# The last down chunk's second token tile in two halves of 256 columns, and both halves of every layer norm centred before either is scaled

## The chip, the cores and the metric

The kernel runs on one core of one Trainium2 chip. The metric is the device time of one execution in microseconds (us). The time before is 1677.98 us, the median of three runs. The engines are TensorE (PE, with its weight loads shown apart as PEld), VectorE (DVE), ScalarE (ACT), GpSimd (POOL) and SyncE (SP), which issues nearly all transfers.

## The reference

Two layers of a decoder trunk work on 256 tokens of 1024 channels in f32. Each layer is a half-step SwiGLU feed-forward network (FFN), a mixer of three parallel branches, and a second half-step FFN. After each of these six stages stands a residual sum with a layer norm:

```
for l in range(DEPTH):
    x = layer_norm(ALPHA * x + 0.5 * swiglu(x, ffn1_up[l], ffn1_down[l]), ln1_g[l], ln1_b[l])
    mix = hybrid_mixer(x, positions, w_in[l], ...)
    x = layer_norm(ALPHA * x + mix, ln2_g[l], ln2_b[l])
    x = layer_norm(ALPHA * x + 0.5 * swiglu(x, ffn2_up[l], ffn2_down[l]), ln3_g[l], ln3_b[l])

def layer_norm(x, gain, bias):
    mu = mean(x); var = mean((x - mu) ** 2)
    return (x - mu) * rsqrt(var + LN_EPS) * gain + bias
```

Up projections have 2 x 2816 columns, down projections go from 2816 channels back to 1024, and the mixer ends in an output projection of 1024 by 1024. The kernel keeps 2x + f and a larger epsilon where the reference has x + 0.5 f, which a layer norm does not tell apart.

## The kernel before

The 256 tokens are two token tiles of 128, `t = 0` and `t = 1`; `x[t]` is 128 tokens by 1024 channels. The weights are cut into chunks of 512 columns, and a chunk into units of up to four blocks of 128 rows (`k`). A unit is loaded (`ws`), rounded on ACT to a high part (`wh`, L280) and its rest taken on DVE as a low part (`wl`, L290), each some 2 us for a full unit. Activations have the same two parts: `xT` and `hT` are pairs of a high and a low tile, channels on partitions. Each product is the sum of three matmuls in fp32r: low by `wh`, high by `wl`, high by `wh`. All of them are issued in `mm_unit` (L321) into an accumulator `acc` of one PSUM bank of 512 columns; three such banks rotate.

`parts` says how a unit is laid out. In the form `tokens`, 128 tokens are the stationary operand and 512 weight columns move; the down and output projections use it. In the form `channels`, 128 weight columns are stationary and the 256 tokens move. A third case is the second half of the chunk `bkv`, which has the form `tokens` with 256 moving columns.

A down projection is two chunks (`n = 0, 1`) of 22 blocks of rows. When the last unit of a chunk is done for a token tile, `done_down` (or `done_out` after the mixer) calls `residual`: x is scaled and the accumulator added (L466), and `bn_stats` takes the statistics of these 512 columns (L467). After `n = 1` it calls `norm`: `bn_aggr` (L472), epsilon (L474), the power -0.5 on POOL (L475), and then for each half of 512 columns two steps: subtract the mean and multiply by the gain (L479), multiply by the power and add the bias (L480). L480 needs the power, L479 does not.

The order of the work is the order of the code; every engine takes its instructions in that order. Between two stages the last W = 3 units are run for tile 0 first, then for tile 1, so that tile 0's norm and transposes lie under tile 1's matmuls. `x_transposes(t)` transposes each half of x on PE (L458, into the bank T for the first 512 channels and S for the second), and `split` makes `xT` of it on ACT (L448) and DVE (L449). Tile 0 is transposed ahead of the last unit of tile 1. Tile 1 is transposed in the middle of the next stage's third unit for tile 0:

```
for u in (s, s + 1):
    self.mm_unit(u, 0)
self.mm_unit(s + 2, 0, lambda: (self.x_transposes(1), self.hi_until(s + W)))
```

After the mixer the last chunk has only two units, since it has eight blocks of rows. So the three last units span two chunks there, and tile 1's residual of the first of them falls on DVE right after tile 0's norm. After the last stage there are no transposes: SP stores each half of each tile of x (L1104) as soon as its L480 is done.

Of the kernel before, what the change touches and what calls it, by code (L numbers as in the profile page):

```python
# [34 lines left out]
F32 = mybir.dt.float32  # L35
# [4 lines left out]
OP = mybir.AluOpType  # L40
# [4 lines left out]
ALPHA = float(np.float32((2.0 * DEPTH) ** 0.25))  # L45
EPS = float(np.float32(1e-5))
# [115 lines left out]
class Kernel:  # L162
# [131 lines left out]
    def mm_unit(self, u, t, mid=None, tick=False):  # L294
        nc = self.nc
        c, k0, n, _ = self.units[u]
        ch = self.chunks[c]
        if ch["ps"][t] is None:
            ch["ps"][t] = self.acc.tile([128, 512], F32, name="acc")
        ps = ch["ps"][t]  # L300
        wh, wl = self.ready[u]
        if k0 == 0 and t == 0:
            if ch["kind"] == "avf" and ch["arg"] == 2:
                assert self.b_done == 4
                self.queue_yT(1, 8)
            elif ch["kind"] == "proj" and ch["arg"] == (1, 1):
                self.queue_yT(2, 8)
            elif ch["kind"] == "gate" and ch["arg"] == (0, 0):
                self.drain()
                self.queue_yT(0, 6)  # L310
        ch["left"][t] -= 1
        parts = self.parts(ch, t)
        for i, (c0, c1, f) in enumerate(parts):
            for k in range(n):
                if mid and k == n // 2:
                    mid()
                pairs = f(k0 + k, wh[:, k], wl[:, k])
                for j, (a, b) in enumerate(pairs):
                    first = k0 + k == 0 and i == 0 and j == 0
                    last = ch["left"][t] == 0 and k == n - 1 and j == 2  # L320
                    nc.tensor.matmul(ps[:, c0:c1], a, b, start=first, stop=last, skip_group_check=len(parts) > 1)  # L321
        if tick:
            self.tick(t)
        if ch["left"][t] == 0:
            getattr(self, "done_" + ch["kind"])(ch, t, ps)
            ch["ps"][t] = None


    def parts(self, ch, t):

        kind = ch["kind"]

        def pairs(k):
            if kind == "down":
                return self.hT[0][:, k], self.hT[1][:, k]
            if kind in ("proj", "out"):
                hi, lo = (self.mT if kind == "out" else self.yT[ch["arg"][0]])[k // 4]
                return hi[:, k % 4], lo[:, k % 4]
            return self.xT[0][:, k], self.xT[1][:, k]

        def tokens(i, order, c0=0, c1=512):
            def f(k, wh, wl):
                h, l = (order(v, i) for v in pairs(k))
                return (l, wh[:, c0:c1]), (h, wl[:, c0:c1]), (h, wh[:, c0:c1])
            return f

        def channels(b):
            def f(k, wh, wl):
                h, l = pairs(k)
                c = slice(128 * b, 128 * b + 128)  # L350
                return (wl[:, c], h), (wh[:, c], l), (wh[:, c], h)
            return f

        nat = lambda v, i: v[:, 128 * i:128 * i + 128]
        if kind in ("cq", "ck", "bq", "aqk", "gate", "proj") or kind == "up" and ch["arg"] > 1 or kind == "bkv" and t == 0:
            return [(256 * b, 256 * b + 256, channels(2 * t + b)) for b in range(2)]
        if kind == "bkv":
            return [(256 * i, 256 * i + 256, tokens(i, nat, 256)) for i in range(2)]
        return [(0, 512, tokens(t, nat))]


    def setup(self):
        nc, a = self.nc, self.a
        self.x = [self.per.tile([128, 1024], F32, name=f"x{t}") for t in range(2)]
        self.ident = self.per.tile([128, 128], F32, name="ident")
        load = lambda t, n: nc.sync.dma_start(self.x[t][:, 512 * n:512 * n + 512],
                                              a["x"][128 * t:128 * t + 128, 512 * n:512 * n + 512])
        nc.scalar.dma_start(self.ident, a["ident"])
        load(0, 0)
        self.dma_early(0, 0)  # L370
        load(0, 1)
        for k in range(1, 4):
            self.dma_early(0, k)
        load(1, 0)
        load(1, 1)
        for v in (1, 2):
            for k in range(4):
                self.dma_early(v, k)
        self.dma_until(self.STAGE - 1)
        self.xT = [self.per.tile([128, 8, 256], F32R, name=f"xT{i}") for i in range(2)]  # L380
        self.mask = self.per.tile([128, 640], F32, name="mask")
        self.sink = self.per.tile([128, DEPTH, HB], F32, name="sink")
        self.nhalf = self.per.tile([128, 8], F32, name="nhalf")
        nc.vector.memset(self.nhalf, -0.5)
        self.cos = self.per.tile([128, 256], F32, name="cos")
        self.sin = self.per.tile([128, 256], F32, name="sin")
        self.gbias = self.per.tile([128, DEPTH, 3, 8], F32, name="gbias")
        self.st = [self.per.tile([128, 2, 6], F32, name=f"st{t}") for t in range(2)]

    def warm_up(self, n):  # L390

# [68 lines left out]
            self.split(sl(self.xT[0]), sl(self.xT[1]), ps)  # L460


    def residual(self, t, n, ps, scale):
        nc = self.nc
        xs = self.x[t][:, 512 * n:512 * n + 512]
        nc.vector.scalar_tensor_tensor(xs, xs, scale, ps, op0=OP.mult, op1=OP.add)  # L466
        nc.vector.bn_stats(self.st[t][:, n], xs)  # L467

    def norm(self, t, eps):
        nc = self.nc  # L470
        mv = self.sml.tile([128, 2], F32, name="mv")
        nc.vector.bn_aggr(mv, self.st[t])  # L472
        rs = self.sml.tile([128, 1], F32, name="rs")
        nc.vector.tensor_scalar(rs, mv[:, 1:2], eps, None, op0=OP.add)  # L474
        nc.gpsimd.tensor_tensor(rs, rs, self.nhalf[:, 0:1], op=OP.pow)  # L475
        for n in range(2):
            sl = slice(512 * n, 512 * n + 512)
            xs = self.x[t][:, sl]
            nc.vector.scalar_tensor_tensor(xs, xs, mv[:, 0:1], self.g[:, sl], op0=OP.subtract, op1=OP.mult)  # L479
            nc.vector.scalar_tensor_tensor(xs, xs, rs, self.b[:, sl], op0=OP.mult, op1=OP.add)  # L480


# [684 lines left out]
```

## Time and profile before

| what | before |
|---|---|
| median of 3 runs (lowest, highest) | 1677.98 us (1677.12, 1678.56) |
| profiled execution: its own time, and its span from first to last instruction | 1677.88 us, 1676.1 us |
| PE busy | 1662.5 us, 99% of the span, 12325 matmuls |
| DVE busy, ACT busy, POOL busy | 63%, 49%, 3% |
| granted TensorE clock, mean | 0.998 of full speed |
| read from memory | 297.31 MB, 178 GB/s |

The own time is 1.78 us longer than the span, which is what lies around the first and the last instruction. Busy PE is a share of time in which some matmul was under way, not of its peak. What the table does not tell is where PE waits in short places and what lies behind its last matmul.

### The profile page before, as it was taken

The numbers are of one execution on the slowest core, as the hardware profiler recorded it, in microseconds if no ns is written. First come the engines' busy times: TensorE is split into PE (matmuls) and PEld (weight loads), VectorE is DVE, ScalarE is ACT, GpSimd is POOL, SyncE is SP. The second block draws the span as 40 slices with busy tenths as digits, with TensorE's granted clock in tenths as the row PEclk, the third lists the DMA queues.
The fourth block names the chain that finished last, engine by engine and source line by source line (L and its number), as shares of the span: only waits on it lengthen the run. The fifth ranks groups of instructions, "written<-read, shape, count | busy, mean of one in ns | idle before, by whom it ended". The sixth has DMA issues, their size and how long they took to land.

```text
span 1676.1 us, 29127 instructions
## 1 busy us (share of the span) xinstructions
PE 1662.5 (99%) x12325; PEld 1530.6 (91%) x12325; DVE 1063.5 (63%) x1532; ACT 829.6 (49%) x1195; POOL 53.7 (3%) x124
## 2 busy tenths in 40 slices
PE   9999999999999999999999999999999999999997
PEld 7998899998999997999889988999989999989986
DVE  5554668878765467545564456788778555674544
ACT  5443343566776644443344344335667864544431
POOL 0000000000111000000000000000001110000000
PEclk9999999999999999999999999999999999999999
DMA  8544554444543454655445455445444534545451
GB/s 291 200 189 189 201 202 171 156 164 158 176 171 137 179 190 176 225 190 193 172 178 224 189 197 196 172 153 188 162 164 165 178 138 169 218 167 226 172 206 51
DMA packets 50674, 303.39 MB, mean 181 GB/s; under 512 B 7024, under 2 KB 10352, under 8 KB 16624
## 3 DMA queue, kind: packets, MB, share of 16 engines
q1 hardware_dynamic: 49248, 297.27, 48.3%
q0 software_dynamic: 1152, 4.19, 0.7%
q8 instruction: 97, 1.59, 0.4%
q14 instruction: 33, 0.27, 0.0%
q10 hardware_dynamic: 144, 0.07, 0.0%
HBM read 297.31 MB, written 1.05 MB: 178 GB/s over the span
## 4 chain that ended last, share of the span: by engine, by line
PE 96%; DVE 2%; issue 1%; ACT 1%; DMA 0%; POOL 0%; POOLq 0%; SPq 0%
PE acc L321 89%; PE S L641 1%; PE S L630 1%; PE U L776 1%; PE U L853 1%; PE T L630 1%; DVE x L480 0%; ACT af L650 0%; DVE wl L290 0%; DMA x<-in_x_dram 0%; PE S L458 0%; PE T L682 0%; PE T L641 0%; POOL rs L475 0%; DVE x L466 0%
## 5 line engine op out<-in xcount | busy, mean ns | idle before, releaser
L321 PE MATMUL acc<-xT,wh 128*128 128x256 f32 x4800 | 843.5, 279 | 0.0
L321 PEld LDWEIGHTS acc<-xT,wh 128*128 128x128 f32 x4800 | 732.0, 188 | 0.5
L290 DVE TENSOR_TENSOR wl<-ws,wh 128x2048 fp32r<-128x2048 f32 (+1 forms) x277 | 614.8, 2239 | 176.7 <-ACT wh L280 176.3
L321 PE MATMUL acc<-xT,wl 128*128 128x256 f32 x2400 | 674.6, 281 | 0.0
L280 ACT ACTIVATE wh<-ws 128x2048 fp32r<-128x2048 f32 (+1 forms) x277 | 519.0, 1875 | 255.6 <-PE acc L321 219.1
L321 PEld LDWEIGHTS acc<-xT,wl 128*128 128x128 f32 x2400 | 451.2, 188 | 3.9 <-issue 2.7
L321 PE MATMUL acc<-wh,xT 128*128 128x512 f32 (+1 forms) x832 | 260.7, 390 | 0.3 <-DVE xT L449 0.3
L321 PE MATMUL acc<-wh,hT 128*128 128x512 f32 x704 | 222.0, 395 | 0.0
L321 PEld LDWEIGHTS acc<-wh,xT 128*128 128x128 f32 x832 | 154.8, 189 | 36.3 <-issue 1.3
L321 PE MATMUL acc<-wl,xT 128*128 128x512 f32 (+1 forms) x416 | 161.3, 388 | 0.0
L321 PEld LDWEIGHTS acc<-wh,hT 128*128 128x128 f32 x704 | 132.7, 188 | 30.5
L321 PE MATMUL acc<-wl,hT 128*128 128x512 f32 x352 | 138.9, 395 | 0.0
L321 PE MATMUL acc<-slab,wh 128*128 128x256 f32 x704 | 126.4, 281 | 0.0
L491 DVE TENSOR_TENSOR h<-sa,acc 128x512 f32<-128x512 f32 x36 | 24.7, 687 | 154.3 <-PE acc L321 149.6
L321 PEld LDWEIGHTS acc<-slab,wh 128*128 128x128 f32 x704 | 108.1, 188 | 0.0
L321 PE MATMUL acc<-slab,wl 128*128 128x256 f32 x352 | 100.5, 286 | 0.0
L488 ACT ACTIVATE sa<-acc 128x512 f32<-128x512 f32 x36 | 21.5, 596 | 158.4 <-PE acc L321 158.4
L321 PEld LDWEIGHTS acc<-wl,xT 128*128 128x128 f32 x416 | 78.5, 189 | 16.2
L321 PEld LDWEIGHTS acc<-wl,hT 128*128 128x128 f32 x352 | 66.3, 188 | 15.2
L321 PEld LDWEIGHTS acc<-slab,wl 128*128 128x128 f32 x352 | 66.3, 188 | 0.8 <-issue 0.7
L650 ACT ACTIVATE an<-an,bnm 128x128 f32<-128x128 f32 x64 | 28.4, 446 | 55.8 <-DVE bnm L816 31.8
L466 DVE SCALAR_TENSOR_TENSOR x<-x,acc 128x512 f32<-128x512 f32 x24 | 16.4, 685 | 53.6 <-PE acc L321 53.6
(190 smaller groups left out, 1233.7 us busy)
## 6 DMA issues: line engine op xcount, KB each, us to landing
ws<-in_w_dram SPq DMA_DIRECT2D x265, 1024.0 KB, 4.9
ws<-in_w_dram SPq DMA_DIRECT2D x12, 512.0 KB, 4.0
ws<-in_w_dram SPq DMA_DIRECT2D x12, 256.0 KB, 5.4
va<-slab SPq DMA_DIRECT2D x96, 32.0 KB, 4.0
gain<-in_ln_g_dram SPq DMA_DIRECT2D x4, 512.0 KB, 5.7
gain<-in_ln_b_dram SPq DMA_DIRECT2D x4, 512.0 KB, 7.2
slab<-in_decay_dram POOLq DMA_DIRECT2D x4, 512.0 KB, 4.6
x<-in_x_dram SPq DMA_DIRECT2D x4, 256.0 KB, 6.1
```

The source lines that it names most:

```text
L280: self.nc.scalar.activation(wh[:, :n], self.staged[v][:, :n], AF.Copy)
L290: self.nc.vector.tensor_tensor(wl[:, :n], ws[:, :n], wh[:, :n].bitcast(F32), op=OP.subtract)
L321: nc.tensor.matmul(ps[:, c0:c1], a, b, start=first, stop=last, skip_group_check=len(parts) > 1)
L466: nc.vector.scalar_tensor_tensor(xs, xs, scale, ps, op0=OP.mult, op1=OP.add)
L488: nc.scalar.activation(self.sa, ps, AF.Silu)
L491: nc.vector.tensor_tensor(h, self.sa, ps, op=OP.mult)
L630: nc.tensor.transpose(ps[:, c + 128 * (i - lo):c + 128 * (i - lo) + 128], P[:, 128 * i:128 * i + 128], self.ident)
L641: self.nc.tensor.matmul(Sp[e][:, 128 * t:128 + 256 * t], q[r, 128 * t:128 * t + 128], k[r, :128 * t + 128], start=True, stop=True)
L650: self.nc.scalar.activation(P, P, AF.Exp, bias=nm, scale=0.125, accum_out=den)
L776: mm = lambda out, v, p, first, last: nc.tensor.matmul(out, v, p, start=first, stop=last, skip_group_check=True)
L853: nc.tensor.matmul(u[:, 128 * j:], v[:, j], P[i][:, e, 256 * j:256 + 128 * j], start=j == 0, stop=j == 1, skip_group_check=True)
```

## The change

Three edits. In the last chunk of the kernel (the second layer's second FFN, down, `n = 1`) tile 1 gets two accumulators of 256 columns each. Every unit of it runs its blocks for the first 256 columns and then for the second. After the last unit's first half, `residual` is called for these 256 columns, and after the second half for the others. `bn_stats` now takes 256 columns at a time everywhere: a residual of 512 columns issues two of them, and `bn_aggr` combines four groups instead of two. And `norm` runs L479 for both halves first, then L480 for both. The second and the third edit apply to all twelve norms.

```diff
--- before.py
+++ after.py
@@ -295,8 +295,9 @@
         nc = self.nc
         c, k0, n, _ = self.units[u]
         ch = self.chunks[c]
+        halves = ch is self.chunks[-1] and t == 1
         if ch["ps"][t] is None:
-            ch["ps"][t] = self.acc.tile([128, 512], F32, name="acc")
+            ch["ps"][t] = [self.acc.tile([128, 512], F32, name="acc") for _ in range(1 + halves)]
         ps = ch["ps"][t]
         wh, wl = self.ready[u]
         if k0 == 0 and t == 0:
@@ -318,11 +319,18 @@
                 for j, (a, b) in enumerate(pairs):
                     first = k0 + k == 0 and i == 0 and j == 0
                     last = ch["left"][t] == 0 and k == n - 1 and j == 2
-                    nc.tensor.matmul(ps[:, c0:c1], a, b, start=first, stop=last, skip_group_check=len(parts) > 1)
+                    if halves:
+                        first = k0 + k == 0 and j == 0
+                    nc.tensor.matmul(ps[i * halves][:, c0:c1], a, b, start=first, stop=last, skip_group_check=len(parts) > 1)
+            if halves and ch["left"][t] == 0:
+                self.residual(1, 2 + i, ps[i], 2.0 * ALPHA, 256)
         if tick:
             self.tick(t)
         if ch["left"][t] == 0:
-            getattr(self, "done_" + ch["kind"])(ch, t, ps)
+            if halves:
+                self.norm(1, 4.0 * EPS)
+            else:
+                getattr(self, "done_" + ch["kind"])(ch, t, ps[0])
             ch["ps"][t] = None
 
 
@@ -352,6 +360,8 @@
             return f
 
         nat = lambda v, i: v[:, 128 * i:128 * i + 128]
+        if ch is self.chunks[-1] and t == 1:
+            return [(256 * i, 256 * i + 256, tokens(t, nat, 256 * i, 256 * i + 256)) for i in range(2)]
         if kind in ("cq", "ck", "bq", "aqk", "gate", "proj") or kind == "up" and ch["arg"] > 1 or kind == "bkv" and t == 0:
             return [(256 * b, 256 * b + 256, channels(2 * t + b)) for b in range(2)]
         if kind == "bkv":
@@ -385,7 +395,7 @@
         self.cos = self.per.tile([128, 256], F32, name="cos")
         self.sin = self.per.tile([128, 256], F32, name="sin")
         self.gbias = self.per.tile([128, DEPTH, 3, 8], F32, name="gbias")
-        self.st = [self.per.tile([128, 2, 6], F32, name=f"st{t}") for t in range(2)]
+        self.st = [self.per.tile([128, 4, 6], F32, name=f"st{t}") for t in range(2)]
 
     def warm_up(self, n):
 
@@ -460,11 +470,12 @@
             self.split(sl(self.xT[0]), sl(self.xT[1]), ps)
 
 
-    def residual(self, t, n, ps, scale):
-        nc = self.nc
-        xs = self.x[t][:, 512 * n:512 * n + 512]
-        nc.vector.scalar_tensor_tensor(xs, xs, scale, ps, op0=OP.mult, op1=OP.add)
-        nc.vector.bn_stats(self.st[t][:, n], xs)
+    def residual(self, t, n, ps, scale, size=512):
+        nc = self.nc
+        xs = self.x[t][:, size * n:size * n + size]
+        nc.vector.scalar_tensor_tensor(xs, xs, scale, ps[:, size * n % 512:size * n % 512 + size], op0=OP.mult, op1=OP.add)
+        for i in range(2 * n, 2 * n + 2) if size == 512 else (n,):
+            nc.vector.bn_stats(self.st[t][:, i], self.x[t][:, 256 * i:256 * i + 256])
 
     def norm(self, t, eps):
         nc = self.nc
@@ -473,10 +484,10 @@
         rs = self.sml.tile([128, 1], F32, name="rs")
         nc.vector.tensor_scalar(rs, mv[:, 1:2], eps, None, op0=OP.add)
         nc.gpsimd.tensor_tensor(rs, rs, self.nhalf[:, 0:1], op=OP.pow)
-        for n in range(2):
-            sl = slice(512 * n, 512 * n + 512)
-            xs = self.x[t][:, sl]
+        halves = [(self.x[t][:, sl], sl) for sl in (slice(0, 512), slice(512, 1024))]
+        for xs, sl in halves:
             nc.vector.scalar_tensor_tensor(xs, xs, mv[:, 0:1], self.g[:, sl], op0=OP.subtract, op1=OP.mult)
+        for xs, sl in halves:
             nc.vector.scalar_tensor_tensor(xs, xs, rs, self.b[:, sl], op0=OP.mult, op1=OP.add)
 
 
```

The first place is DVE at the end of the mixer, tile 0 (`x_78`) and the first residual of tile 1 (`x_79`). Before:

```order
L466 SCALAR_TENSOR_TENSOR x_78<-x_78,acc 128x512
L467 BN_STATS st_116<-x_78 128x6
L472 BN_AGGR mv<-st_116 128x2
L474 TENSOR_SCALAR rs<-mv 128x1
L479 SCALAR_TENSOR_TENSOR x_78<-x_78,mv,slab 128x512
L480 SCALAR_TENSOR_TENSOR x_78<-x_78,rs,slab 128x512
L479 SCALAR_TENSOR_TENSOR x_78<-x_78,mv,slab 128x512
L480 SCALAR_TENSOR_TENSOR x_78<-x_78,rs,slab 128x512
L466 SCALAR_TENSOR_TENSOR x_79<-x_79,acc 128x512
L467 BN_STATS st_117<-x_79 128x6
L290 TENSOR_TENSOR wl<-ws,wh 128x2048
L449 TENSOR_TENSOR xT_108<-T,xT_107 128x4x128
```

The same place in the changed kernel, whose line numbers are up to eleven higher:

```order
L476 SCALAR_TENSOR_TENSOR x_78<-x_78,acc 128x512
L478 BN_STATS st_116<-x_78 128x6 x2
L483 BN_AGGR mv<-st_116 128x2
L485 TENSOR_SCALAR rs<-mv 128x1
L489 SCALAR_TENSOR_TENSOR x_78<-x_78,mv,slab 128x512 x2
L491 SCALAR_TENSOR_TENSOR x_78<-x_78,rs,slab 128x512 x2
L476 SCALAR_TENSOR_TENSOR x_79<-x_79,acc 128x512
L478 BN_STATS st_117<-x_79 128x6 x2
L290 TENSOR_TENSOR wl<-ws,wh 128x2048
L459 TENSOR_TENSOR xT_108<-T,xT_107 128x4x128
```

The second centring step has moved ahead of the first scaling step, and a second `bn_stats` stands behind each first one; nothing else has moved there.

The second place is DVE behind the last matmul, tile 1, in the changed kernel; before, it is the first eight rows above with `x_79`.

```order
L476 SCALAR_TENSOR_TENSOR x_79<-x_79,acc 128x256
L478 BN_STATS st_117<-x_79 128x6
L476 SCALAR_TENSOR_TENSOR x_79<-x_79,acc 128x256
L478 BN_STATS st_117<-x_79 128x6
L483 BN_AGGR mv<-st_117 128x2
L485 TENSOR_SCALAR rs<-mv 128x1
L489 SCALAR_TENSOR_TENSOR x_79<-x_79,mv,gain_15413 128x512 x2
L491 SCALAR_TENSOR_TENSOR x_79<-x_79,rs,gain_15414 128x512 x2
```

The first residual of 256 columns and its `bn_stats` now stand ahead of the second pair.

The third place is PE in the middle of the last unit of tile 1, where the first accumulator (`acc_16415`) ends and the second begins:

```order
L324 MATMUL acc_16415<-wh_16482,hT1_15014 128x256
L324 MATMUL acc_16415<-wl_16483,hT0_15013 128x256
L324 MATMUL acc_16415<-wh_16482,hT0_15013 128x256
L324 MATMUL acc_16416<-wh_16482,hT1_15014 128x256
L324 MATMUL acc_16416<-wl_16483,hT0_15013 128x256
L324 MATMUL acc_16416<-wh_16482,hT0_15013 128x256
```

Before, each of the 22 blocks was three matmuls of 512 columns; now it is three of 256 columns for each half, so 66 matmuls have become 132, each with its own weight load.

## Rows read from the trace of the kernel before

**Rows 1.** The page's chain of work that ended last, shares of the span by engine.
```profile
PE 96%; DVE 2%; issue 1%; ACT 1%; DMA 0%; POOL 0%; POOLq 0%; SPq 0%
```
**Rows 2.** PE's weight loads, whom they waited for: us in total, times, longest us.
```profile
PEld acc L321 <- DVE xT L449: 1.2, 2, 0.6
PEld S L458 <- DVE x L480: 0.8, 2, 0.4
```
**Rows 3.** Timeline, PE, from mixer to FFN (layer 0): start us, us, engine, line.
```profile
650.14 0.39 PE L321 MATMUL acc<-wh,slab 128*128 128x512 f32 x1
650.68 0.50 PE L321 MATMUL acc<-wh,xT 128*128 128x512 f32 x1 [0.16 <-DVE xT L449]
651.02 0.39 PE L321 MATMUL acc<-wl,xT 128*128 128x512 f32 x1
...
657.31 0.40 PE L321 MATMUL acc<-wl,xT 128*128 128x512 f32 x1
...
657.78 0.60 PE L458 MATMUL T<-ident,x 128*128 128x128 f32 x4
...
658.96 0.48 PE L321 MATMUL acc<-wh,xT 128*128 128x512 f32 x1
```
**Rows 4.** Timeline, DVE and PE, tile 1 from first FFN to mixer.
```profile
201.51 0.75 DVE L480 SCALAR_TENSOR_TENSOR x<-x,rs,gain 128x512 f32<-128x512 f32 x1 [0.45 <-POOL rs L475]
...
203.45 0.60 PE L458 MATMUL T<-ident,x 128*128 128x128 f32 x4
...
204.25 0.48 PE L321 MATMUL acc<-wh,xT 128*128 128x512 f32 x1
```
**Rows 5.** Timeline, DVE, from mixer to FFN: tile 0, then tile 1's last step.
```profile
643.10 0.74 DVE L479 SCALAR_TENSOR_TENSOR x<-x,mv,slab 128x512 f32<-128x512 f32 x1
...
646.43 0.68 DVE L466 SCALAR_TENSOR_TENSOR x<-x,acc 128x512 f32<-128x512 f32 x1
...
649.94 0.68 DVE L449 TENSOR_TENSOR xT<-T,xT 128x512 fp32r<-128x512 f32 x1
...
657.74 0.75 DVE L480 SCALAR_TENSOR_TENSOR x<-x,rs,slab 128x512 f32<-128x512 f32 x1
```
**Rows 6.** Timeline behind the last matmul: tile 1's residual and norm on DVE and POOL.
```profile
1666.77 0.69 DVE L466 SCALAR_TENSOR_TENSOR x<-x,acc 128x512 f32<-128x512 f32 x1 [3.22 <-PE acc L321]
1667.49 0.69 DVE L467 BATCH_NORM_STATS2 st<-x 128x6 f32<-128x512 f32 x1
1668.22 0.21 DVE L472 BATCH_NORM_AGGREGATE mv<-st 128x2 f32<-128x12 f32 x1
...
1668.54 0.74 DVE L479 SCALAR_TENSOR_TENSOR x<-x,mv,gain 128x512 f32<-128x512 f32 x1
1668.70 0.99 POOL L475 TENSOR_TENSOR rs<-rs,nhalf 128x1 f32<-128x1 f32 x1 [7.38 <-DVE rs L474]
1669.72 0.75 DVE L480 SCALAR_TENSOR_TENSOR x<-x,rs,gain 128x512 f32<-128x512 f32 x1 [0.44 <-POOL rs L475]
1670.39 0.74 DVE L479 SCALAR_TENSOR_TENSOR x<-x,mv,gain 128x512 f32<-128x512 f32 x1
1671.16 0.75 DVE L480 SCALAR_TENSOR_TENSOR x<-x,rs,gain 128x512 f32<-128x512 f32 x1
```
**Rows 7.** Groups of one line each: duration ns min/median/max, first and last start us, forms.
```profile
L952 DVE BATCH_NORM_STATS2 cst<-y x32: 258/260/287, 271.2 to 1126.6; 128x6 f32<-128x128 f32 x32
...
L428 DVE SCALAR_TENSOR_TENSOR ang<-n,ang x4: 414/424/427, 93.9 to 95.3; 128x256 f32<-128x256 f32 x4
...
L321 PEld LDWEIGHTS acc<-wh,hT x704: 187/188/193, 134.1 to 1666.1; 128*128 128x128 f32 x176
```
**Rows 8.** Timeline, PE, 256 moving columns in the form tokens (bkv, layer 1).
```profile
1108.32 0.28 PE L321 MATMUL acc<-wl,xT 128*128 128x256 f32 x1
...
1110.81 0.28 PE L321 MATMUL acc<-wl,xT 128*128 128x256 f32 x1
```
**Rows 9.** Transfers, busy share in tenths from 1670 to 1675 us, 0.125 us a digit.
```profile
DMA  0000000000299999200000889996101000000000
```

## The prediction

> **What bounds the kernel now.** I read the chain of work that ended last first: 96% of the span is PE [rows 1]. So the time changes only where PE waits inside the run, or in what stands behind its last matmul. The change touches the norms and the last chunk, so I asked which of PE's waits name a norm. There are two kinds, each met twice, once in each layer [rows 2]: matmuls that wait for the low part of `xT` (L449), and the transposes of the second half of x into S, which wait for L480. The timeline puts both at the passage from the mixer to the second FFN [rows 3].
>
> The first: between the starts at 650.14 and 651.02 lie 0.88 us where two matmuls of 512 columns take 2 x 0.233 = 0.47 (9 blocks of three matmuls from 651.02 to 657.31 give 6.29 / 27 = 0.233). So 0.41 us is lost. The second: from the first transpose into T to the first matmul behind the S transposes it is 1.18 us (657.78 to 658.96), and 0.80 at a passage without a wait [rows 4]. So 0.38 us is lost. Together that is 0.79 us a layer, 1.58 us in the run, all behind DVE. At the other three passages PE meets no such wait.
>
> At the end [rows 6] DVE starts the last residual at 1666.77 and ends the last L480 at 1671.91: 5.14 us in which nothing else runs, then the last transfer.
>
> **The norm's new order.** L479 does not need the power, L480 does. Before, DVE stood idle 0.44 us ahead of the first L480 and then ran L479, L480 for the second half [rows 6]. From the first L479 (1668.54) to the end of the last L480 (1671.91) it took 3.37 us. Two such steps that do not depend on each other start 0.67 us apart (1669.72, 1670.39). In the new order all four do: the power is there 1.15 us after the first L479 starts (1668.70 + 0.99 - 1668.54), and the first L480 starts at 2 x 0.67 = 1.34. So the norm ends at 3 x 0.67 + 0.75 = 2.76, 0.61 us earlier. The first half is the loser: it ends at 1.34 + 0.75 = 2.09 where it was 1.93, 0.16 us later.
>
> **The split statistics.** No row shows `bn_stats` on 256 columns. On 128 it takes 0.26 [rows 7], on 512 0.69 [rows 6]; a straight line between gives 0.405. Two are 0.81, so 0.12 us more. But two neighbours that do not depend on each other overlap by 0.08 (0.75 long, 0.67 apart), which leaves 0.04. I take 0.04 and keep 0.12. `bn_aggr` on four groups has no row: it lies between the 0.21 of two groups and twice that; I take 0.10 more and keep 0 and 0.21. Seven of the twelve norms end under PE's matmuls, as shown below; the four of the mixers and the last one are in the sums.
>
> **From mixer to FFN.** DVE works through tile 0's norm, tile 1's first residual, a weight split, and then the `xT` for which PE waits, without a pause but the one for the power [rows 5]. From the first L479 (643.10) to the residual (646.43) it was 3.33 us and becomes 4 x 0.67 = 2.68: 0.65 earlier. Against it stand 0.04 and 0.10 for tile 0's statistics and 0.04 for tile 1's. L449 at 649.94 comes 0.47 earlier, at worst (0.12, 0.10, 0.12) 0.31. PE lost 0.41, so the first wait goes, at worst 0.10 us of it stays.
>
> What is late next is tile 1. Its norm starts 0.47 - 0.14 = 0.33 earlier and ends a further 0.61 earlier: the second half of x is ready at 658.49 - 0.94 = 657.55. PE, now 0.41 earlier, begins the T transposes at 657.37 and, about half of the 0.80 us on, the S ones at 657.77. That holds with 0.2 us in hand, so the second wait goes too. The first half of x was ready at about 657.05 (the last L480's start less 1.44 as in rows 6, plus 0.75) and becomes 0.33 - 0.16 = 0.17 earlier, 656.88, ahead of 657.37. Sum: 2 x (0.41 + 0.38) = **1.58 us**, at worst 2 x (0.31 + 0.38) = 1.38.
>
> The later first half must also hold at the other passages. In rows 4 it is ready at 202.26, with statistics and order some 0.30 later, and PE comes to it at 203.45. The cover is 0.9 us; were it gone, each tenth would cost a tenth.
>
> **The last chunk on PE.** 66 matmuls of 512 columns become 132 of 256. The nearest rows are the same form with 256 moving columns [rows 8]: seven blocks in 2.49 us, 2.49 / 21 = 0.1186 for one. Two make 0.2372 against 0.2330: 0.0042 a pair, 66 x 0.0042 = **0.28 us** more. The other end is exact halves, nothing. [...]
>
> The second accumulator must be free when tile 1 comes to its second half in the chunk's first unit. It was read by the 0.69 us residual of the chunk before; since then PE has issued six matmuls of tile 0 (1.4 us) and six of the first half (0.7 us). That covers it; without the cover it would be at most 0.7 us, once.
>
> **Behind the last matmul.** The first half's residual and statistics (0.42 by the same operation on 256 columns [rows 7], and 0.405) lie under the twelve matmuls of the last unit's second half (12 x 0.1186 = 1.42), with DVE idle 3.22 us before [rows 6]. What is left behind the last matmul is 0.69 - 0.42 = 0.27 shorter in L466 and 0.69 - 0.405 = 0.28 in the statistics, 0.10 longer in `bn_aggr`, 0.61 shorter in the norm: 1.06 us. The two last transfers ran apart, each 0.85 us of nearly full engines [rows 9], the second from 0.84 us after its L480. Now they are issued 0.67 apart, so the second waits up to 0.18; I take 0.18 and keep 0. The end gains 1.06 - 0.18 - 0.28 = **0.60 us**.
>
> **Sum.** 1.58 + 0.60 = 2.18 us off the profiled execution's own 1677.88: 1675.7. The median is 0.10 above that execution, less than the three runs differ.
>
> **Rivals.**
> A: the waits in the mixer do not give time back. DVE, which runs earlier, then waits for ACT's high part of a weight, or PE merely stops at the next thing it needs. For it: tile 1's S transposes have 0.2 us in hand only. Against it: the loads and splits are released by the same DVE queue, which is earlier too. Then only the end gains: 1677.3.
> B: the end gains nothing: the last transfer lands no earlier, or the 256-column matmuls cost 0.9 us in place of 0.28, 0.013 a pair. Then 1677.88 - 1.58 = 1676.3.
> C, slower: a weight load takes 0.188 us [rows 7], and if the loads stand alone, 66 more cost 12.4 us: 1677.88 - 2.18 - 0.28 + 12.4 = 1687.8. It decides from 0.037 us a pair on, where both gains are eaten. Against it: in rows 8 each matmul has its own load and they start every 0.1186 us, less than one load lasts. [...]
>
> **Chances.** The forecast 0.77, A 0.12, B 0.08, C 0.03. The best ends of the unknown costs (1.58 and 1.16) give 1675.1, and the three runs lie up to 0.9 from their median, so the range begins at 1674.5; it reaches to A at 1677.3, and leaves out C and some spread at either end. A measurement of this kernel can tell about 0.2%, 3.4 us, from no change. Only the low tail of the forecast lies below 1674.6: faster 0.07. Slower is C and a little more, 0.04. The same 0.89.
>
> **What would show it.** In the changed profile no weight load of PE waits for L459 or L491; T to first matmul takes 0.80 at both mixers; the first L491 has no idle time before it; the last residual to the end of the last L491 takes about 4.1 us where it was 5.14; the last chunk's tile 1 has blocks of about 0.711 us for six matmuls. The forecast is wrong if those waits stay, if six take over 0.73, or if the last transfer still moves data more than 2 us after its L491.

## The result, and the profile after

The changed kernel is slower: 1685.85 us (median of six runs, 1685.54 to 1687.62) against 1677.99 us for six runs of the kernel before beside it, a ratio of 1.0051, with a 95% interval of 1.0041 to 1.0061. The forecast was 1675.7 us, its range ended at 1677.3, and "slower" had a chance of 0.04. The profiled execution has a span of 1683.8 us, where it was 1676.1, at a granted clock of 0.999.

What is strange is that each step that the prediction spoke of happened. I read the same places in the same order. First the page's chain of work that ended last, by engine [rows 1], and the weight loads of PE that waited for DVE in the list of waits [rows 2]:

```profile
PE 98%; ACT 1%; DMA 0%; DVE 0%; issue 0%; SPq 0%; DVEq 0%
```
```profile
PEld T L996 <- DVE slab L459: 1.7, 2, 0.9
...
PEld acc L324 <- DVE wl L459: 0.5, 1, 0.5
```

DVE is gone from the chain. L459 is what L449 was and L491 what L480 was: no load waits for the `xT` of L459 or for the x of L491 any more. Of the two rows with L459 that are left, `T L996` is a wait inside the mixer that was there before (`T L985`, 1.8 us in all), and `wl` is one at the start of the kernel, 9.4 us in. The timeline of PE at the passage from mixer to FFN [rows 3]:

```profile
653.99 0.39 PE L324 MATMUL acc<-wh,slab 128*128 128x512 f32 x1
654.22 0.39 PE L324 MATMUL acc<-wh,xT 128*128 128x512 f32 x1
654.45 0.39 PE L324 MATMUL acc<-wl,xT 128*128 128x512 f32 x1
...
661.21 0.60 PE L468 MATMUL T<-ident,x 128*128 128x128 f32 x4
...
662.00 0.48 PE L324 MATMUL acc<-wh,xT 128*128 128x512 f32 x1
```

From the last `slab` matmul to the second of `xT` it is 0.46 us, two matmuls and no gap (0.88 before), and from the T transposes to the first matmul behind the S ones 0.79 (1.18 before). DVE at the same passage [rows 5]:

```profile
645.90 0.75 DVE L478 BATCH_NORM_STATS2 st<-x 128x6 f32<-128x256 f32 x2
646.69 0.26 DVE L483 BATCH_NORM_AGGREGATE mv<-st 128x2 f32<-128x24 f32 x1
646.99 0.15 DVE L485 TENSOR_SCALAR rs<-mv 128x1 f32<-128x1 f32 x1
647.06 1.41 DVE L489 SCALAR_TENSOR_TENSOR x<-x,mv,slab 128x512 f32<-128x512 f32 x2
648.38 1.41 DVE L491 SCALAR_TENSOR_TENSOR x<-x,rs,slab 128x512 f32<-128x512 f32 x2
649.71 0.68 DVE L476 SCALAR_TENSOR_TENSOR x<-x,acc 128x512 f32<-128x512 f32 x1
```

No idle time stands before L491, and the four steps take 2.65 us where they took 3.33 (forecast 2.68). And the end [rows 6], PE's last matmuls and then DVE:

```profile
1673.07 0.28 PE L324 MATMUL acc<-wl,hT 128*128 128x256 f32 x1
...
1676.28 0.28 PE L324 MATMUL acc<-wl,hT 128*128 128x256 f32 x1
1676.40 0.28 PE L324 MATMUL acc<-wh,hT 128*128 128x256 f32 x1
```
```profile
1676.72 0.42 DVE L476 SCALAR_TENSOR_TENSOR x<-x,acc 128x256 f32<-128x256 f32 x1 [0.54 <-PE acc L324]
...
1679.33 1.41 DVE L491 SCALAR_TENSOR_TENSOR x<-x,rs,gain 128x512 f32<-128x512 f32 x2
```

From the last residual to the end of the last L491 it is 4.02 us, where it was 5.14. Nine triples of 256 columns take 3.21 us, so six matmuls 0.713 (forecast 0.711). Behind L491 it is 3.06 us to the end of the span, where it was 4.19: the two last transfers, which ran apart [rows 9], now run in one stretch (1676 to 1684 us, 0.2 us a digit), and SP's queue, which before waited 2.3 us for the last of them, now waits 0.6 us twice (before, then after):

```profile
DMA  0000000000000000000000002999999600000000
```
```profile
SPq L1163 <- DMA out_dram<-x: 2.3, 1, 2.3
```
```profile
SPq L1174 <- DMA out_dram<-x: 1.2, 2, 0.6
```

From the start of the last matmul to the end of the span it is 7.40 us, and it was 9.76 (1676.1 - 1666.34, its row in the trace of before).

So the time was lost somewhere else. The page's costliest group of PE tells where, first before, then after:

```profile
L321 PE MATMUL acc<-xT,wh 128*128 128x256 f32 x4800 | 843.5, 279 | 0.0
```
```profile
L324 PE MATMUL acc<-xT,wh 128*128 128x256 f32 x4800 | 854.6, 281 | 0.0
```

This group is 11 us longer. With the 2400 `wl` matmuls beside it, it holds the matmuls of the form `channels` that read `xT`: 2400 triples (two with `wh`, one with `wl`) of 256 moving tokens, 1152 of them in the up projections and the others in the mixers. The diff doesn't touch them. In the timeline of the first up projection, before and then after, each row with `wl` marks one triple:

```profile
60.02 0.28 PE L321 MATMUL acc<-xT,wl 128*128 128x256 f32 x1
...
65.97 0.28 PE L321 MATMUL acc<-xT,wl 128*128 128x256 f32 x1
```
```profile
59.73 0.28 PE L324 MATMUL acc<-xT,wl 128*128 128x256 f32 x1
...
65.77 0.28 PE L324 MATMUL acc<-xT,wl 128*128 128x256 f32 x1
```

Both stretches hold 17 triples: 5.95 / 17 = 0.350 us before, 6.04 / 17 = 0.355 after. There is no wait in either; every matmul merely starts 1.8 ns later. The triples of the mixers are slower in both (0.353 and 0.358). Added up over the starts of all 7200 matmuls in the two traces it is 11.0 us. The down projections, whose weights and activations the change moves together, start 0.9 ns later each (232.4 and 233.3 ns), another 0.9 us. With -1.6 at the mixers and -1.9 at the end (7.40 - 9.76, with the 0.12 by which the last matmul has become shorter and the 0.3 for the halves of the last chunk added) that makes +8.4, and +7.9 is measured.

### The profile page after: what moved, and what is told of

Its sections match the earlier page's. It is cut to its first block, busy times and chain, and to the rows that moved or that the text cites. A ratio compares the mean times of both kernels' runs of the same rounds, so it can differ in the third digit from the quotient of the medians.

```text
span 1683.8 us, 29284 instructions
## 1 busy us (share of the span) xinstructions
PE 1672.7 (99%) x12391; PEld 1542.5 (92%) x12391; DVE 1064.2 (63%) x1557; ACT 829.5 (49%) x1195; POOL 53.9 (3%) x124
## 3 DMA queue, kind: packets, MB, share of 16 engines
q0 software_dynamic: 1152, 4.19, 0.8%
## 4 chain that ended last, share of the span: by engine, by line
PE 98%; ACT 1%; DMA 0%; DVE 0%; issue 0%; SPq 0%; DVEq 0%
PE acc L324 92%; PE S L652 1%; PE S L641 1%; PE U L787 1%; PE U L864 1%; PE T L641 1%; ACT af L661 0%; DMA ws<-in_w_dram 0%; PE T L693 0%; PE T L652 0%; PE T L468 0%; PE S L468 0%; ACT wh L280 0%; PE T L518 0%; PE T L996 0%; PE S L934 0%
## 5 line engine op out<-in xcount | busy, mean ns | idle before, releaser
L324 PE MATMUL acc<-xT,wh 128*128 128x256 f32 x4800 | 854.6, 281 | 0.0
L324 PE MATMUL acc<-wh,hT 128*128 128x512 f32 (+1 forms) x748 | 224.3, 382 | 0.0
L324 PEld LDWEIGHTS acc<-wh,hT 128*128 128x128 f32 x748 | 137.5, 188 | 29.7
L324 PE MATMUL acc<-wl,hT 128*128 128x512 f32 (+1 forms) x374 | 142.7, 382 | 0.0
L324 PEld LDWEIGHTS acc<-wl,hT 128*128 128x128 f32 x374 | 70.3, 188 | 14.8
L476 DVE SCALAR_TENSOR_TENSOR x<-x,acc 128x512 f32<-128x512 f32 (+1 forms) x25 | 16.6, 664 | 53.2 <-PE acc L324 53.2
```

Source lines behind the costliest of these rows:

```text
L324: nc.tensor.matmul(ps[i * halves][:, c0:c1], a, b, start=first, stop=last, skip_group_check=len(parts) > 1)
L476: nc.vector.scalar_tensor_tensor(xs, xs, scale, ps[:, size * n % 512:size * n % 512 + size], op0=OP.mult, op1=OP.add)
```

## The experiments

**What could slow a matmul that was not edited?** Theory P: its operands lie elsewhere. The diff widens the statistics tiles `st` from 48 to 96 bytes a partition (64 to 96 with the padding that the program gives them). They are allocated behind `xT` and ahead of the weights, so all that comes later moves by 64 bytes. The places in the two programs, bytes in a partition (this is no profile):

```
        before   after
xT0      25216   25216
st0      46560   46560
wh       71264   71328
hT0     138976  139040
```

All `wh` and `wl` buffers lie whole multiples of 8192 apart, and so do the two `xT`, so one number says it: the distance from the weights to `xT`, modulo 256, is 32 before and 224 after. Rival I: the added instructions (weight loads, statistics, another order on DVE) slow PE. Parts of the change alone tell them apart.

**Wide statistics tiles alone.** The kernel before, none of its instructions changed.

```diff
-        self.st = [self.per.tile([128, 2, 6], F32, name=f"st{t}") for t in range(2)]
+        self.st = [self.per.tile([128, 4, 6], F32, name=f"st{t}") for t in range(2)]
...
-        nc.vector.bn_aggr(mv, self.st[t])
+        nc.vector.bn_aggr(mv, self.st[t][:, :2])
```

> The kernel before, and only the statistics tiles have the new size of 128 x 4 x 6; half of each stays unused. Every tile that is allocated behind them (ws, wh, wl, hT, slab) lies 64 bytes further on in a partition, as in the changed kernel; no instruction is added or reordered. Theory P (placement: the 256-column matmuls start later one after the other because weights and activations lie otherwise to each other): three matmuls of the up chunks take 0.355 us in place of 0.350, and with 2400 such triples the time is 1688 to 1691 us. Rival I (the added or reordered instructions slow PE everywhere): 1678 us, as before.

1689.19 us, ratio 1.0070 (1.0056 to 1.0084), and the page's group is that of after to the digit:

```profile
L321 PE MATMUL acc<-xT,wh 128*128 128x256 f32 x4800 | 854.6, 281 | 0.0
```

**The whole change, with the old places.** 192 unused bytes bring the distance back to 32.

```diff
         self.st = [self.per.tile([128, 4, 6], F32, name=f"st{t}") for t in range(2)]
+        self.pad = self.per.tile([128, 48], F32, name="pad")
```

> The changed kernel with an unused tile of 192 bytes behind the statistics tiles, so that everything behind lies 256 bytes further on than in the kernel before. Theory P, if places count modulo 256 bytes: triples of 0.350 us again, and what the forecast named is left, 1674 to 1676 us. Rival I: 1685 to 1686 us, as the changed kernel. If places count over a longer distance than 256 bytes, something between or above.

1674.10 us, ratio 0.9982 (0.9973 to 0.9991): 3.3 us under the 1677.39 of before beside it, and the group is back:

```profile
L324 PE MATMUL acc<-xT,wh 128*128 128x256 f32 x4800 | 843.6, 279 | 0.0
```

Rival I falls with these two: the placement alone costs 11.8 us, and the instructions alone save 3.3; together +8.5 against the +7.9 measured.

**Another 64 bytes**, so that the distance is 160.

```diff
+        self.pad = self.per.tile([128, 16], F32, name="pad")
```

> The changed kernel with an unused tile of 64 bytes behind the statistics tiles: everything behind lies 128 bytes further on than in the kernel before. Theory P, places modulo 128 bytes: 1674 to 1676 us; places modulo 256 bytes: not as before, 1680 us or more. Rival I: 1685 to 1686 us.

1685.61 us, ratio 1.0049 (1.0036 to 1.0063); a triple takes 0.356. So 128 bytes further on is not as good as the old place; 256, in the kernel with 192 bytes, was.

**The new order of the norm alone**, on the kernel before, with its statistics and its last chunk as they were.

```diff
-        for n in range(2):
-            sl = slice(512 * n, 512 * n + 512)
-            xs = self.x[t][:, sl]
+        halves = [(self.x[t][:, sl], sl) for sl in (slice(0, 512), slice(512, 1024))]
+        for xs, sl in halves:
             nc.vector.scalar_tensor_tensor(xs, xs, mv[:, 0:1], self.g[:, sl], op0=OP.subtract, op1=OP.mult)
+        for xs, sl in halves:
             nc.vector.scalar_tensor_tensor(xs, xs, rs, self.b[:, sl], op0=OP.mult, op1=OP.add)
```

> The kernel before with the norm's new order alone: L479 for both halves, then L480; statistics, tiles and the last chunk as before, so nothing is moved in memory. By the steps of the forecast 2 x 0.79 us of waits in the mixers and 0.6 us at the end go: 1675.8 us. If the waits are not given back, 1677.4. Theory P and rival I say nothing against 1675.8 here, except that under I a mere reordering on DVE could slow PE: then 1680 or more.

1675.44 us, ratio 0.9988 (0.9979 to 0.9996): 2.0 us less.

**Is it the distance or the place?** Two kernels move things without a change of instructions. One adds 64 bytes ahead of everything (`pad0` as below, with `[128, 16]`): all places change, no distance does. The other adds 192 bytes ahead of everything and 64 behind `st`: the weights are back at their old place modulo 256, and `xT` has moved against them (distance 224). In the second:

```diff
+        self.pad0 = self.per.tile([128, 48], F32, name="pad0")
         self.x = [self.per.tile([128, 1024], F32, name=f"x{t}") for t in range(2)]
...
         self.st = [self.per.tile([128, 2, 6], F32, name=f"st{t}") for t in range(2)]
+        self.pad = self.per.tile([128, 16], F32, name="pad")
```

> The kernel before with an unused tile of 64 bytes ahead of all others: weights, xT and hT all lie 64 bytes further on, and their places to each other are as before. Theory P relative (what counts is how far the moving operand lies from the stationary one, modulo 256 bytes): 1677 to 1678 us, as before. Theory P absolute (what counts is where the weights lie themselves): 1688 to 1691, as with the wide statistics tiles.

> The kernel before with an unused tile of 192 bytes ahead of all others and one of 64 behind the statistics tiles: the weights lie 256 bytes further on, so modulo 256 where they were, xT 192 bytes. To each other xT and weights lie as in the changed kernel. Theory P relative: 1688 to 1691 us. Theory P absolute by the weights' place: 1677 to 1678 us.

1677.73 us, ratio 1.0000 (0.9991 to 1.0009), and 1688.99 us, 1.0067 (1.0051 to 1.0082). The page's group is 843.5 in the first and 854.6 in the second. It is the distance.

**The halves and the statistics alone**: the changed kernel with the old order of the norm and the old distance.

```diff
+        self.pad = self.per.tile([128, 48], F32, name="pad")
...
-        halves = [(self.x[t][:, sl], sl) for sl in (slice(0, 512), slice(512, 1024))]
-        for xs, sl in halves:
+        for n in range(2):
+            sl = slice(512 * n, 512 * n + 512)
+            xs = self.x[t][:, sl]
             nc.vector.scalar_tensor_tensor(xs, xs, mv[:, 0:1], self.g[:, sl], op0=OP.subtract, op1=OP.mult)
-        for xs, sl in halves:
             nc.vector.scalar_tensor_tensor(xs, xs, rs, self.b[:, sl], op0=OP.mult, op1=OP.add)
```

> The changed kernel with the norm in its old order and the unused 192 bytes that bring everything back modulo 256: the halves and the split statistics alone. By the forecast's terms: mixers lose 0.04 to 0.12 us of statistics and 0.10 of aggregation each time, PE 0.28 us, the end gains 0.27 + 0.28 - 0.10 = 0.45: 1677.2 to 1678.2 us, no change that can be measured. If the tail's unforeseen gain (its last transfer) comes with the halves, 1676.

1677.12 us, ratio 0.9997 (0.9988 to 1.0006), 0.6 us less, which this comparison can't tell from nothing.

This kernel and the one with the new order alone also show with which part the short last transfer at the end came. SP's queue waits for the transfers, first with the new order of the norm alone, then with the halves and the old order:

```profile
SPq L1163 <- DMA out_dram<-x: 2.4, 2, 1.8
```
```profile
SPq L1175 <- DMA out_dram<-x: 1.2, 1, 1.2
```

In the first the two are issued 0.67 us apart, and the last lands 3.21 us after its issue (3.18 before). In the second they are 1.45 us apart, as before, and it lands after 2.01. So it isn't the short distance in time. It goes with the halves: in eight traces with them SP's queue waits 1.2 us in all for these transfers, in five without them 2.3 or 2.4. In the trace of before one packet of the instruction queue (q14, 8 KB) runs at the end of the transfer, from 1673.78 to 1674.09 us; in that of after none does. Whether that packet holds it up was not tried.

**All distances in steps of 32.** The changed kernel with this line, and with 40, 24, 32 and 56 in the place of 8:

```diff
+        self.pad = self.per.tile([128, 8], F32, name="pad")
```

> The changed kernel with an unused tile of 160 bytes: the weights lie 224 bytes further on than before, and xT lies 64 bytes after them modulo 256 where it was 32 in the kernel before. No value is known for this distance. Theory P says only that the up chunks' triples and the time move together: 1674 us at 0.350 us, 1686 at 0.355, and each 0.001 us of a triple is 2.4 us.

> The changed kernel, weights 96 bytes further on than in the kernel before: xT lies 192 bytes after them modulo 256. Known so far: 32 bytes 1674.1 us, 64 bytes 1680.0, 160 bytes 1685.6, 224 bytes 1685.9. No value is known for 192. Theory P relative: the time follows the up chunks' triples by 2.4 us for each 0.001 us; between the neighbours 160 and 224, so 1684 to 1687.

> The changed kernel, weights 160 bytes further on: xT lies 128 bytes after them modulo 256. In the gate chunks' neighbours, the projections, slab tiles lie 128 bytes from the weights in every kernel so far, at 0.357 to 0.360 us a triple. Theory P relative: the up chunks now take that too, 1688 us or more.

> The changed kernel, weights 192 bytes further on: xT lies 96 bytes after them modulo 256. Between 64 bytes (1680.0 us) and 128: if the cost grows with the distance, 1682 to 1686 us.

> The changed kernel, weights 288 bytes further on: xT and the weights lie at the same place modulo 256. Operands at the same place could meet worst, 1688 us or more, or, if 32 bytes is good because it is near, as well as 32: 1674.

Two of the sizes that I had guessed were wrong by far: 192 is not like its neighbours, it is the best of all, and 96 is the worst. The table has all kernels that differ in this distance; a triple is read from the timeline between 60 and 66 us.

| distance, bytes | triple, us | changed kernel, us | kernel before, us |
|---|---|---|---|
| 192 | 0.340 | 1653.16 (pad 32) | 1656.57 (below) |
| 32 | 0.350 | 1674.10 (pad 192) | 1677.99 |
| 64 | 0.353 | 1680.03 (pad 160) | |
| 224 | 0.355 | 1685.85 (the change) | 1689.19, 1688.99 |
| 160 | 0.356 | 1685.61 (pad 64) | |
| 128 | 0.360, 0.356 | 1688.40 (pad 96) | 1692.35 (below) |
| 0 | 0.360 | 1690.19 (pad 224) | |
| 96 | 0.360 | 1697.52 (pad 128) | |

The ratios to before are 0.9850 (0.9821 to 0.9879) at 192, 1.0015 (1.0004 to 1.0025) at 64, 1.0061 (1.0038 to 1.0084) at 128, 1.0073 (1.0050 to 1.0096) at 0 and 1.0114 (1.0085 to 1.0144) at 96. At 96 and at 0 the triples are alike, and the kernels differ by 7.3 us. That lies in another form that reads `xT`, 1152 matmuls of 512 moving columns with `xT` stationary (first at 96, then at 0; their `wl` rows differ by another 2.4):

```profile
L324 PE MATMUL acc<-wh,xT 128*128 128x512 f32 x768 | 248.9, 398 | 0.0
```
```profile
L324 PE MATMUL acc<-wh,xT 128*128 128x512 f32 x768 | 244.2, 393 | 0.6 <-ACT wh L459 0.6
```

By their starts one takes 234 ns at 96, 233 at 32, 229 at 192 and 227 at 0, so this form ranks the distances in another way. At 192, 18 triples of the same up projection take 6.12 us:

```profile
59.81 0.28 PE L324 MATMUL acc<-xT,wl 128*128 128x256 f32 x1
...
65.93 0.28 PE L324 MATMUL acc<-xT,wl 128*128 128x256 f32 x1
```

**Is the gain at 192 the placement's alone?** The kernel before with nothing but unused bytes behind `st`. The first try, 160 bytes, had an error of sign: more bytes there make the distance smaller.

```diff
         self.st = [self.per.tile([128, 2, 6], F32, name=f"st{t}") for t in range(2)]
+        self.pad = self.per.tile([128, 40], F32, name="pad")
```

> The kernel before, with 160 unused bytes per partition behind the statistics tiles and nothing else, so that the distance from the rounded weights to xT is 192 bytes (modulo 256), as in the kernel after with 32 unused bytes, which took 1653.2 us. Theory (the distance alone sets the pitch of the channel triples): a mean pitch of 114.1 ns in place of 116.9, and the 24.9 us less that the other kernel showed, without the 3.3 us that the halves and the new order of the norm give: 1656 to 1657 us. Rival (the gain at 192 needs the added instructions or another order of them): 1670 to 1678 us.

1692.35 us, ratio 1.0084 (1.0069 to 1.0099): it lies at 128, and fits that row, not the one it was meant for. The second try has `[128, 24]`, 96 bytes:

> The kernel before with 96 unused bytes per partition behind the statistics tiles and nothing else. The expectation of the kernel with 160 bytes had an error of arithmetic: each byte added there lessens the distance from the weights to xT, so 32 - 160 is 128 modulo 256, not 192; its 1692.4 us are those of the changed kernel at 128 (1688.4) and the 3.3 us of the halves and the norm. At 96 bytes the distance is 32 - 96 = 192 modulo 256. Theory (the distance alone sets the pitch): 1653.2 + 3.3 = 1656 to 1657.5 us, and a mean pitch of 114.1 ns. Rival (the gain at 192 needs the added instructions): 1670 us or more.

1656.57 us, ratio 0.9873 (0.9857 to 0.9890), 0.340 us a triple. So 21 us come from 96 bytes that nobody reads.

**Do the down projections feel it too?** There `hT` is stationary and the weights move, and `hT` lay 128 beyond them in all kernels so far. Two kernels move `hT` and the tiles behind it, not `xT` or the weights, the first by 64 bytes to 192, the second by 192 bytes (`[128, 48]`) to 64:

```diff
+            self.hpad = self.fp.tile([128, 16], F32, name="hpad")
             self.hT = [self.fp.tile([128, 22, 256], F32R, name=f"hT{i}") for i in range(2)]
```

> The kernel before, with 64 unused bytes per partition ahead of hT, so that the distance from hT (stationary in the down projections) to the rounded weights that move is 64 bytes modulo 256 where it is 128; xT and the up projections keep theirs. The down projections are 1056 matmuls of 512 columns at 232 to 233 ns. Theory that the law of the channel triples holds for moving minus stationary in every form: a distance of 64 is 1.2 ns a matmul better than 128 there, so 1 to 3 us less, 1675 to 1677 us. Rival (512 moving columns, or the tokens as stationary operand, do not feel the distance): 1677.5 to 1678.5 us.

> The kernel before, with 192 unused bytes per partition ahead of hT, so that the distance from hT to the weights is 192 bytes modulo 256, the best one for the channel triples (114.1 ns against 118.9 at 128). Theory that the same law holds in every form: 4.8 to 9.6 ns off each of 1056 matmuls, 5 to 10 us less, 1668 to 1673 us. Rival (that form does not feel it): 1677.5 to 1678.5 us. If it is the distance with the other sign that counts, this kernel and the one with 64 bytes change places.

1674.21 us, ratio 0.9979 (0.9970 to 0.9988), and 1678.09 us, 1.0002 (0.9992 to 1.0012). The theory missed both sizes, the second fits its rival, and the good one is the other one. The groups of the down projections, before (in order: with `wh`, with `wl`) and then with `hT` at 192:

```profile
L321 PE MATMUL acc<-wh,hT 128*128 128x512 f32 x704 | 222.0, 395 | 0.0
...
L321 PE MATMUL acc<-wl,hT 128*128 128x512 f32 x352 | 138.9, 395 | 0.0
```
```profile
L321 PE MATMUL acc<-wh,hT 128*128 128x512 f32 x704 | 219.6, 391 | 0.0
...
L321 PE MATMUL acc<-wl,hT 128*128 128x512 f32 x352 | 138.0, 392 | 0.0
```

They are 2.4 and 0.9 us shorter, 3.3 of the 3.5 us of the run. So the form feels it, less: 3.9 us lie between the three places tried (64, 128, 192), and 35.2 between the same three of `xT` in the changed kernel. Here too the one 192 beyond the weights was the best.

**Do the two gains add?** The changed kernel with `pad` of 32 bytes and `hpad` of 64, so that `xT` and `hT` both lie 192 beyond the weights.

> The changed kernel with 32 unused bytes behind the statistics tiles and 64 ahead of hT: xT and hT both lie 192 bytes modulo 256 beyond the weights. Theory (the two forms feel their own distances, and the gains add): the 1653.2 us of 32 bytes alone less the 3.5 us that hT gave the kernel before: 1649 to 1650.5 us. Rival (the gain of hT in the kernel before was of another kind, or PE is no longer the bound at the up projections): 1652.5 us or more.

```diff
+        self.pad = self.per.tile([128, 8], F32, name="pad")
...
+            self.hpad = self.fp.tile([128, 16], F32, name="hpad")
```

1662.25 us, ratio 0.9907 (0.9893 to 0.9922): 9 us slower than without `hpad`. The theory failed; the rival's range (1652.5 or more) holds the time, but neither of its reasons gives a loss of 9 us. The timeline shows one more thing, six triples of the first FFN of layer 0, and then six of the first FFN of layer 1, with all operands at the same places:

```profile
109.84 0.28 PE L324 MATMUL acc<-xT,wl 128*128 128x256 f32 x1
...
111.88 0.28 PE L324 MATMUL acc<-xT,wl 128*128 128x256 f32 x1
```
```profile
929.93 0.28 PE L324 MATMUL acc<-xT,wl 128*128 128x256 f32 x1
...
932.05 0.28 PE L324 MATMUL acc<-xT,wl 128*128 128x256 f32 x1
```

2.04 / 6 = 0.340 and 2.12 / 6 = 0.353. Without `hpad` both FFNs run at 0.340 (113.3 ns a matmul in either). In this kernel the first FFN of layer 0 is fast and that of layer 1 is not. There the down projections are slower too; here are six matmuls of them in the first FFN of layer 0, and then six in the first of layer 1:

```profile
150.03 0.39 PE L324 MATMUL acc<-wl,hT 128*128 128x512 f32 x1
...
151.40 0.39 PE L324 MATMUL acc<-wl,hT 128*128 128x512 f32 x1
```
```profile
980.11 0.40 PE L324 MATMUL acc<-wl,hT 128*128 128x512 f32 x1
...
981.51 0.40 PE L324 MATMUL acc<-wl,hT 128*128 128x512 f32 x1
```

That is 228 and 233 ns a matmul. So the distance does not settle the pitch by itself: here it has one value in one stage and another in the other, and what chooses is open.

## Why the prediction was wrong

- **The bound** was read rightly: PE sets the end, and only PE's waits and the end can change the time. What was missing is a third way: PE's own pace, 0.350 us a triple before and 0.355 after. Busy PE stayed at 99%, and the only new waits of PE are 0.7 us at the start of the kernel, where another is 0.4 shorter, so no view of waits could show it; the means of groups and the starts of like matmuls did.
- **The norm's new order** was right: 2.65 us against 2.68, no idle time before L491, and by itself 2.0 us off the run. The forecast has 1.58 for the mixers and 0.61 for the end, 2.2.
- **The split statistics** were right as a term of DVE: two cost 0.75 us in place of 0.69 (forecast 0.04 more, with 0.12 as bound), `bn_aggr` 0.26 in place of 0.21 (forecast 0.10 more). **The step that failed stands in this part**: the edit was priced by its instructions alone. It also made two tiles larger, which moved every weight buffer by 64 bytes against `xT`, and that costs 11.8 us with no instruction added (the wide tiles alone).
- **From mixer to FFN** was right: both waits are gone in the trace, and nothing took their place. Rival A, that the time is not given back, is out.
- **The last chunk on PE** was right: 0.713 us for six matmuls, 66 x (0.713 - 0.699) / 3 = 0.3 us. Rival C gave nearly the measured time (1687.8) by a mechanism that did not occur: each of these matmuls has its own load of 0.19 us, and they start every 0.119, so the loads stay hidden. That its number came near is chance.
- **Behind the last matmul** the sign was right and the size too small. The work on DVE is 1.12 us shorter (forecast 1.06). The transfers, booked as a loss of 0.18, gave another 1.13. No step of the forecast has that gain; it came with the halves and not with the shorter time between the two transfers, and why is open. Rival B is out.
- **The sum** of what was counted comes to 1674.1 in the changed kernel with the old places, 1.6 us from the forecast and just below its range. The halves and the statistics gave 0.6 us of it alone, the order of the norm 2.0; that the two make 2.6 and not the 3.3 of both together lies within the intervals. So the sum without the placement came out near, with 1.13 us in it that was not forecast.
- **The chances** had no case for a cause outside the edited instructions; 0.04 for slower held rival C and a little more. None of its three signs of being wrong came; all of them looked at the edited places.

## What to carry to other kernels

An edit that changes the size of a tile can move the tiles behind it, as `st` moved all weight buffers by 64 bytes here: compare the addresses of the stationary and the moving operands of the costliest matmuls before and after, and compare the pitch of matmuls that the edit doesn't touch. To judge an edit by itself, pad until the old places are back; to tune, try the offsets: in this kernel 96 unused bytes were worth 21 us, some six times the 3.3 us of the edit. Such an offset has to be tried in the final kernel, since the next move of another tile can take the gain away, as `hpad` did (1653.16 us became 1662.25).

## What the runs showed of the hardware

- The pitch of 256-column matmuls with a fresh weight load each, at a granted clock of 0.997 to 0.999, was 0.340 to 0.360 us a triple, 113 to 120 ns for one, by the distance of the two operands in a partition, modulo 256 (the period was tried at 32 only: the changed kernel with 192 unused bytes, 256 further on than before). Moving all tiles together by 64 bytes changed nothing (1677.73 us, ratio 1.0000). The distance does not say all: two values were seen at 192 (0.340, and 0.353 in the kernel with `pad` and `hpad`) and at 128 (0.360 in the changed kernel, 0.356 in the kernel before).
- The same instructions differ by 44 us between the best and the worst offset (the changed kernel, 1653.16 us at 192 and 1697.52 at 96). Where in the memory or in PE the offset acts, no run here shows.
- Two `bn_stats` of 256 columns that follow each other took 0.75 us (the changed kernel), one of 512 took 0.69 (the kernel before).
- Still open: why 192 is best and 96 worst of the eight distances (1653.16 and 1697.52 us), why 512 columns with `xT` stationary were fastest at 0 of the four read (227 ns), and what made a stage of the last kernel run at 0.353 with the places that ran at 0.340. It wasn't tried to move `hT` and what lies behind it apart.
